# A convolution's first stage written six sweep products later, each of its groups ordered behind the last sweep product

## The chip, the cores and the metric

The kernel runs on one core of one Trainium2 chip. The metric is the device time of one execution in microseconds (us). A comparison with the kernel before is made of runs of both on the same chip.

## What is computed

One layer of a hybrid encoder, for 2048 positions of 1024 channels. RMSNorm and one input projection feed two groups of heads: a long convolution (three streams of 512 channels) and an mLSTM. Their outputs are joined and projected; a cross attention over 256 memory rows and a squared-ReLU network follow. The change touches the convolution:

```python
def _hyena(hy, spec, skip):
    L = hy.shape[1]
    u = hy.astype(jnp.float32)
    z, g1, g2 = u[..., :D_HYENA], u[..., D_HYENA:2 * D_HYENA], u[..., 2 * D_HYENA:]
    for o, gate in enumerate((g1, g2)):
        conv = jnp.fft.irfft(jnp.fft.rfft(z, n=2 * L, axis=1) * spec[:, o], n=2 * L, axis=1)[:, :L]
        z = gate * (conv + z * skip[o].astype(jnp.float32))
    return z

def reference(x, mem, ...):
    u = _rms_norm(h, norm_mix_g[l])
    proj = u @ w_in[l]
    hy = _short_conv_centred(proj[..., :HY_COLS], hy_conv_w[l], hy_conv_b[l])
    spec = _hyena_filter_spectrum(L, ...)
    y_hy = _group_rms_norm(_hyena(hy, spec, hy_skip[l]), hy_norm_g[l], HYENA_GROUPS)
    ...
```

## The kernel before

The input projection runs in "sweeps": a sweep product is a block of 128 output columns by 512 positions, eight blocks of the inner dimension, three matmuls each (`mm3`: high by high, high by low and low by high parts of x, `xh`/`xl`, and of the weights, `wh`/`wl`), so 24 matmuls on TensorE (PE, lines 351, 354, 355). "Natural" tiles do the same with the roles exchanged, for the values and gates. The weights come through SP's queue (`wn`, line 391) and are split on ACT and DVE (line 362). Half of the positions is done first; then x is scaled and split again for the other half (`xt` loads, line 492).

The convolution is a Fourier transform in matmuls, in four stages. The two convolutions, o=0 and o=1, have the same stages:

- First stage, `spectrum`: for each of eight pieces j2, two pairs of matmuls with the constant `f1` (a pair uses both halves of the array; `beside`, lines 177 and 188), copied out (line 918 and its neighbour) and written to the memory tensor `zs` (line 920; one half on SP's queue, the other on ACT's). The input `z` comes from `hy` (line 851).
- Blocks, i = 0 to 15: `zs` is read back across (line 868), with the filter's tile from `fs` (line 860). `response` makes the filter's values (line 875, into the bank `mm`); the data go through `dm` (line 948, into the bank `hy`), are multiplied by the response on ACT, POOL and DVE (lines 950 to 954), and `back` (line 906, by `em`) follows, one item late; the result is written to `zg` (line 910, ACT's queue).
- Inverse: `zg` is read back (line 890) with the gate (line 893), multiplied by `e2` (line 177 through `beside`), and by the gate on DVE (line 968). For o=0 the next first stage follows at once, one item late; for o=1 a norm, then a write to `yh`.

Who stands where: the program is one Python thread, and the framework's scheduler takes, on each engine, among the instructions that it deems ready, the one written first, except where an order is pinned. Each engine then runs its queue in that fixed order, and waits there for what its instruction needs. The order in which the code is written is set by generators: `weave(a, b, wa, wb)` takes turns between the convolution `p.hyena` (weight 279) and the sweeps (weight 499); each `yield` tells how much work the piece behind it is (a sweep product 5.5, a first-stage piece 3.5, a block 4.6). `p.hyena` begins with `yield 6` ahead of its first piece.

`beside` writes the matmuls of a pair: the last one is made first and, with `pin`, kept in program order among the pinned instructions; the others get a high priority and a pinned place. `mm3` keeps the last matmul of a sweep product in `self.last`, and `behind(ins)` adds an order dependency (no semaphore) on it: `ins` may not be put on PE ahead of that matmul. In the kernel before, the filters' opening uses `behind`; `spectrum` does not.

In what follows, a number of sweep matmuls is the count of projection matmuls that PE's queue holds ahead of an instruction.

Of the kernel before, what the change touches and what calls it, by code (L numbers as in the profile page):

```python
# [133 lines left out]
class Prog:  # L134
# [38 lines left out]
    def beside(self, *products, pin=False):  # L173
        names = [p[0].tensor.name for p in products]
        n = min(self.banks.index(t) for t in names)
        held = self.banks[max(0, n - 4):max(0, n - 2)] if len(set(names)) > 1 else []
        b = self.nc.tensor.matmul(*products[-1], start=True, stop=True)  # L177
        if pin:
            self.tc.keep_in_program_order(b)
        for i in reversed(self.nc.cur_bb.bb.instructions[-4000:]):  # L180
            own = [x.bass_ap.tensor.name for x in i.ins if getattr(x, "bass_ap", None) is not None]
            for t in [t for t in held if t in own]:
                held.remove(t)
                self.tc.add_manual_dep(b.ins, i.name, mybir.DependencyInfo(
                    mybir.DependencyClass.Sync, mybir.DependencyReason.DATA), reason="beside")
        with self.tc.high_priority(2000):
            for p in reversed(products[:-1]):
                self.tc.keep_in_program_order(self.nc.tensor.matmul(*p, start=True, stop=True))
# [633 lines left out]
    def hyena(self, es):  # L822
# [6 lines left out]
        own = [slice(64 * g, 64 * g + 64) for g in range(2)]  # L829
# [6 lines left out]
        def ta():  # L836
            return sb.tile([128, 2, CH], F32, tag="a", name="a", bufs=10)
# [4 lines left out]
        f1 = sb.tile([128, 128], F32, name="f1")  # L842
# [4 lines left out]
        def load1(j2):  # L847
            z = ta()
            js = slice(2 * j2, 2 * j2 + 2)
            for g in range(2):  # L850
                nc.sync.dma_start(out=z[own[g]], in_=hy[0, g, :, js])
            return z
# [59 lines left out]
        def spectrum(o, j2, z):  # L912
            st = [ta() for p in range(2)]
            for jj in range(2):
                pp = [self.hy() for b in range(2)]
                self.beside(*((pp[g], f1[own[g]], z[own[g], jj]) for g in range(2)), pin=True)
                for b in range(2):
                    (nc.vector.tensor_copy if b else nc.scalar.copy)(st[b][:, jj], pp[b])
            for b in range(2):
                (nc.sync if b else nc.scalar).dma_start(out=sds[o][b, :, 2 * j2:2 * j2 + 2], in_=st[b])  # L920

        q, fq = [load1(0), load1(1)], []
        yield 6
        for j2 in range(8):
            yield 3.5
            if j2 < 6:
                q.append(load1(j2 + 2))
            else:
                fq.append(load_filter(0, j2 - 6))
            spectrum(0, j2, q.pop(0))  # L930
        for o in range(2):
# [4 lines left out]
            for i in range(16):  # L936
# [9 lines left out]
                for m in range(2):  # L946
                    pp = self.hy()
# [11 lines left out]
            for j2 in range(8):  # L959
                yield 4.5 if o else 6.0  # L960
                js = slice(2 * j2, 2 * j2 + 2)
                r, gate = nxt
                if j2 < 7:
                    nxt = load3(o, j2 + 1)
                for jj in range(2):
                    pp = self.hy()
                    self.beside(*((pp[own[g]], e2, r[g][:, jj]) for g in range(2)), pin=jj == 0)
                    nc.vector.tensor_tensor(gate[:, jj], pp, gate[:, jj], ALU.mult)
                if o == 0:
                    late(lambda j2=j2, gate=gate: spectrum(1, j2, gate))  # L970
                    if j2 > 5:
                        fq.append(load_filter(1, j2 - 6))
                    continue
                y = gate.rearrange("q j (g e) -> q (j g) e", g=8)
                sq = ta()
                sqv = sq.rearrange("q j (g e) -> q (j g) e", g=8)
                nc.gpsimd.tensor_tensor(sqv, y, y, ALU.mult)
                ms = sb.tile([128, 16], F32, tag="ms", name="ms", bufs=2)
                nc.vector.tensor_reduce(ms, sqv, AX.X, ALU.add)
                rv = self.bank_rsqrt(sb, ms, 64)  # L980
                nc.vector.tensor_tensor(sqv, y, rv.unsqueeze(2).broadcast_to([128, 16, 64]), ALU.mult)
                for jj in range(2):
                    nc.gpsimd.tensor_tensor(sq[:, jj], sq[:, jj], ghy, ALU.mult)
                for g in range(2):
                    nc.sync.dma_start(out=yh[g, :, js], in_=sq[own[g]])
# [954 lines left out]
def chain(*gens):  # L1940
    for g in gens:
        yield from g


def weave(a, b, wa, wb, until=False):
    da = db = 0.0
    fa = fb = False
    while not (fa and fb):
        if fb or (not fa and da / wa <= db / wb):
            try:  # L1950
                da += next(a)
            except StopIteration:
                fa = True
        else:
            try:
                db += next(b)
            except StopIteration:
                fb = True
                if until:
                    return  # L1960


def program(p):
    with ExitStack() as ms:
        with ExitStack() as es:
            p.inproj_open(es)
            p.filters_open()
            p.prepq = p.x_first()
            p.pop()
            s = chain(p.sweep(range(4), 0, True, lambda: p.prep_x(1)), p.opened(), p.sweep(range(4), 1, False))  # L1970
            f = p.filters()
            for _ in range(5):
                next(s)
            next(f)
            next(f)
            next(s)
            weave(s, f, 140, 102, True)
            p.gates_open(ms)
            n = p.memproj()
            with ExitStack() as hs:  # L1980
                weave(p.hyena(hs),
                      chain(s, p.sweep(range(4, 10), 1, True), p.natural(1, (3, 0, 1, 2), lambda: p.prep_x(0)),
                            p.natural(0, (3,)), among(p.sweep((4, 5, 8, 9), 0, False), p.gates(), 2),
                            among(chain(p.natural(0, (0, 1)), p.sweep((6, 7), 0, False),
                                        p.natural(0, (2,), p.prep_mem, 2), take(n, 3)), p.states(), 1)),
                      279, 499)
            m = p.mlstm(ms)
            weave(n, take(m, 5), 55, 30)
            for _ in take(m, 1):
                pass  # L1990
        with ExitStack() as rs:
            p.ts = rs.enter_context(ExitStack())
            p.tail_open(p.ts)
            with ExitStack() as at:
                g = p.attention(at)
                weave(g, m, 440, 96, True)
                ms.close()
                p.ffn_open(rs)
                for _ in g:
                    pass  # L2000
            p.ffn()


def among(g, h, every):
    for i, v in enumerate(g):
        yield v
        if i % every == every - 1:
            next(h, None)
    for _ in h:
        pass  # L2010


def take(g, n):
    for _ in range(n):
        v = next(g, None)
        if v is None:
            return
        yield v
# [31 lines left out]
```

## Time and profile before

| what | value |
|---|---|
| runs before, us | 3146.3, 3149.82, 3152.24 (median 3149.82) |
| profiled execution, us | 3143.82 |
| its span, us | 3142.1 |
| mean granted TensorE clock | 0.984 of full speed |
| DMA traffic | 607.13 MB, mean 193 GB/s |

In the profile's lines a name is the program's, without its buffer number; an arrow points from what is read to what is written; L351 is line 351. "SPq" and "ACTq" are the DMA-issuing queues of these engines. In the chain of waits each row is a start, a length and what the end of the program hung on at that time. In a timeline a bracket tells how long the engine stood idle ahead of the row, and which instruction's end let it go on. Matmuls overlap: a 128x512 row takes 0.39 to 0.43 us from start to end, but the next begins 0.23 us after it.

### The profile page before, as it was taken

What the parts mean: (1) busy time and instruction counts of PE and PEld (TensorE: products, weight loads), DVE (VectorE), ACT (ScalarE), POOL (GpSimd) and SP (SyncE); (2) the same over time, 40 slices, a digit from 0 to 9 for tenths busy, and PEclk for the clock granted to TensorE, in tenths of its full rate; (3) what the DMA queues carried; (4) which work ended last, traced back from release to release, by engine and by line L of the source; (5) the groups of instructions that cost most, each with busy time, mean ns of one, the idle gap of its engine ahead of it and who ended that gap; (6) DMA issues with size and microseconds to landing.
All of it is one profiled execution on the core that took longest, in us unless ns stands there. A gap on an engine that the chain in (4) does not pass through costs nothing.

```text
span 3142.1 us, 43602 instructions
## 1 busy us (share of the span) xinstructions
PE 3030.6 (96%) x14481; PEld 2390.2 (76%) x14481; DVE 2049.6 (65%) x3569; ACT 1493.9 (48%) x2848; POOL 1161.9 (37%) x802
## 2 busy tenths in 40 slices
PE   8999999999999977999999999999999999999998
PEld 6655566876687767888887888888888778888876
DVE  7965456446646778877765656557555685555695
ACT  5443366534646345454544455556555443333335
POOL 0122012100222244324141327776456393434493
PEclk9999999999999988999999999999999999999999
DMA  6564767586777987455385647656644574434424
GB/s 212 153 209 164 260 192 214 171 253 216 215 217 233 279 274 254 147 181 196 113 282 165 234 154 245 208 184 225 207 154 151 172 238 144 151 124 152 124 91 171
DMA packets 446667, 607.13 MB, mean 193 GB/s; under 512 B 39007, under 2 KB 249055, under 8 KB 445417
## 3 DMA queue, kind: packets, MB, share of 16 engines
q1 hardware_dynamic: 408548, 546.54, 54.5%
q10 hardware_dynamic: 37892, 57.79, 5.5%
q8 instruction: 115, 1.88, 0.2%
q14 instruction: 112, 0.91, 0.1%
HBM read 401.79 MB, written 202.41 MB: 192 GB/s over the span
## 4 chain that ended last, share of the span: by engine, by line
PE 79%; DMA 8%; DVE 6%; issue 3%; ACT 2%; POOL 1%; SPq 1%; ACTq 0%; DVEq 0%; POOLq 0%
PE mm L351 17%; PE mm L355 17%; PE mm L354 17%; PE hy L355 5%; PE hy L351 5%; PE hy L354 5%; PE hy L177 3%; PE mm L875 2%; PE hy L906 2%; PE hy L948 2%; DMA a<-hy 1%; PE hy L1112 1%; DVE wl L362 1%; PE hy L1235 1%; DVE bl L1580 1%
## 5 line engine op out<-in xcount | busy, mean ns | idle before, releaser
L362 DVE TENSOR_TENSOR wl<-wn,wh 128x512 fp32r<-128x512 f32 (+1 forms) x364 | 285.9, 828 | 120.8 <-ACT wh L362 120.3
L1580 DVE TENSOR_TENSOR bl<-wr,bh 128x512 fp32r<-128x512 f32 x213 | 240.4, 1136 | 132.3 <-ACT bh L1579 132.2
L1579 ACT CAST ah<-w 128x512 fp32r<-128x512 f32 x284 | 177.1, 624 | 301.9 <-PE hy L354 154.5
L953 POOL TENSOR_TENSOR b<-b,a 128x512 f32<-128x512 f32 x64 | 88.5, 1383 | 533.7 <-ACT b L951 507.9
L351 PE MATMUL mm<-xh,wh 128*128 128x512 f32 x640 | 272.9, 427 | 11.2 <-ACT wh L362 9.1
L362 ACT CAST wh<-wn 128x512 fp32r<-128x512 f32 (+1 forms) x364 | 205.3, 620 | 154.6 <-PE mm L355 51.8
L1579 ACT CAST bh<-wr 128x512 fp32r<-128x512 f32 x232 | 143.9, 622 | 237.3 <-PE mm L355 172.6
L355 PE MATMUL mm<-xh,wl 128*128 128x512 f32 x640 | 256.5, 401 | 0.0
L354 PE MATMUL mm<-xl,wh 128*128 128x512 f32 x640 | 255.1, 399 | 0.7 <-DVE xl L362 0.6
L1580 DVE TENSOR_TENSOR al<-w,ah 128x512 fp32r<-128x512 f32 x236 | 215.3, 913 | 54.1 <-ACT ah L1579 54.0
L355 PE MATMUL mm<-bh,al 128*128 128x512 f32 x576 | 224.7, 393 | 6.0 <-DVE al L1580 3.4
L351 PE MATMUL mm<-bh,ah 128*128 128x512 f32 x576 | 226.5, 393 | 2.2 <-DVE acc L1737 2.2
L354 PE MATMUL mm<-bl,ah 128*128 128x512 f32 x576 | 225.7, 392 | 0.0
L351 PE MATMUL mm<-act,wh 128*128 128x512 f32 x512 | 199.2, 395 | 2.1 <-ACT wh L362 2.0
L354 PE MATMUL mm<-act,wh 128*128 128x512 f32 x512 | 200.4, 392 | 0.2 <-DVE act L362 0.2
L355 PE MATMUL mm<-act,wl 128*128 128x512 f32 x512 | 199.7, 392 | 0.9 <-DVE wl L362 0.6
L351 PE MATMUL hy<-bh,ah 128*128 128x512 f32 x448 | 175.2, 391 | 0.0
L354 PE MATMUL hy<-bl,ah 128*128 128x512 f32 x448 | 174.6, 390 | 0.0
L355 PE MATMUL hy<-bh,al 128*128 128x512 f32 x448 | 174.4, 390 | 0.0
L351 PEld LDWEIGHTS mm<-xh,wh 128*128 128x128 f32 x640 | 121.9, 191 | 66.6 <-issue 23.5
L334 POOL TENSOR_TENSOR b<-b 128x512 f32<-128x512 f32 x32 | 58.3, 1823 | 277.2 <-DVE b L331 137.6
L354 PEld LDWEIGHTS mm<-xl,wh 128*128 128x128 f32 x640 | 121.9, 191 | 48.8 <-issue 22.6
(380 smaller groups left out, 8479.3 us busy)
## 6 DMA issues: line engine op xcount, KB each, us to landing
wr<-hc SPq DMA_DIRECT2D x224, 256.0 KB
w<-in_ff_w_dram SPq DMA_DIRECT2D x172, 256.0 KB
hc<-wn SPq DMA_DIRECT2D x128, 256.0 KB
wn<-in_w_in_dram SPq DMA_DIRECT2D x100, 256.0 KB
hc<-q SPq DMA_DIRECT2D x96, 256.0 KB
fs<-a SPq DMA_DIRECT2D x32, 512.0 KB
a<-fs SPq DMA_DIRECT2D x64, 256.0 KB
a<-zs SPq DMA_DIRECT2D x64, 256.0 KB
```

What stands on the lines that cost most here:

```text
L177: b = self.nc.tensor.matmul(*products[-1], start=True, stop=True)
L334: nc.gpsimd.tensor_tensor(e[1], f, b, ALU.subtract)
L351: first = mm(ps, lh, rh, start=start, stop=False)
L354: mm(ps, lh, rl, start=False, stop=False)
L355: self.last = mm(ps, ll, rh, start=False, stop=stop)
L362: both = (self.nc.scalar.copy(hi, src), self.nc.vector.tensor_tensor(lo, src, hi.bitcast(F32), ALU.subtract))
L875: nc.tensor.matmul(pp, dm[:, m], t[:, m], start=True, stop=True)
L906: nc.tensor.matmul(pg, em[:, m], y, start=True, stop=True)
L948: nc.tensor.matmul(pp, dm[:, m], t[:, m], start=True, stop=True)
L953: nc.gpsimd.tensor_tensor(xt, xt, hi[:, m], ALU.mult)
L1579: self.nc.scalar.copy(hi, src)
L1580: eng.tensor_tensor(lo, src, hi.bitcast(F32), ALU.subtract)
```

## The change

```diff
@@ beside
         if pin:
             self.tc.keep_in_program_order(b)
+        if pin == 2:
+            self.behind(b)
@@ hyena
-                self.beside(*((pp[g], f1[own[g]], z[own[g], jj]) for g in range(2)), pin=True)
+                self.beside(*((pp[g], f1[own[g]], z[own[g], jj]) for g in range(2)), pin=1 if o else 2)
...
         q, fq = [load1(0), load1(1)], []
-        yield 6
+        yield 24
@@ program
-                      279, 499)
+                      297, 499)
```

The first stage of the first convolution (o=0) gets the order dependency: the last-written matmul of each pair stands behind the last sweep product that was written ahead of it. The convolution's first piece is written 18 units of its own measure later, and its weight in `weave` goes up by the same 18, so that its end stays beside the same place of the sweeps. No instruction is added or removed on PE, DVE, POOL or the queues; ACT loads an activation table two times more (for Silu and Sigmoid). In the changed kernel all lines from 180 on have a number higher by 2.

On PE, rows differ from sweep matmul 939 to the start of the mLSTM, and nowhere else. The sixteen pairs of the first stage stood in ten places between sweep matmuls 939 and 1021; now they stand two by two at 939, 960, 984, 1008, 1032, 1056, 1080 and 1104. The first response (line 875) stood at 1008, ahead of the last two pairs, and the first line 948 at 1056; now they stand at 1104, right behind the last two pairs, and at 1176. The later blocks of o=0 come 96 to 264 sweep matmuls later, the inverse of o=0 begins at 2165 instead of 2016, the last first-stage piece of o=1 stands at 2579 instead of 2520, the last inverse of o=1 at 3906 instead of 3890.

SP's queue at the handover from first stage to blocks, before (`zs` is the first stage's result, `fs` the filter, `qt` a result of the sweep):

```order
L851 DMA a<-hy 64x1024 x2
L920 DMA zs_2574<-a 128x1024
L757 DMA hy<-st 126x4x128 x2
L860 DMA a<-fs_354 64x2x512 x2
L920 DMA zs_2574<-a 128x1024
L860 DMA a<-fs_354 64x2x512 x2
L920 DMA zs_2574<-a 128x1024 x2
L868 DMA a<-zs_2574 64x2x512 x2
```

and after the change:

```order
L922 DMA zs_2574<-a 128x1024
L768 DMA qt<-cv 128x1008
L393 DMA wn<-in_w_in_dram 128x2x256
L862 DMA a<-fs_354 64x2x512 x2
L393 DMA wn<-in_w_in_dram 128x2x256 x3
L922 DMA zs_2574<-a 128x1024
L768 DMA qt<-cv 128x1008
L862 DMA a<-fs_354 64x2x512 x2
L922 DMA zs_2574<-a 128x1024 x2
```

In both, the first load of `fs` stands behind the fifth write of `zs`; weight loads and a write of `qt` now stand around it, where two writes of `hy` stood.

SP's queue where the inverse of o=0 (`zg`, with its gate from `hy`) meets the loads of x for the other half (`xt`), before:

```order
L890 DMA a<-zg_2576 128x1024 x2
L893 DMA a<-hy 64x1024 x2
L890 DMA a<-zg_2576 128x1024 x2
L893 DMA a<-hy 64x1024 x2
L391 DMA wn<-in_w_in_dram 128x2x256 x4
L890 DMA a<-zg_2576 128x1024 x2
L893 DMA a<-hy 64x1024 x2
L492 DMA xt<-in_x_t_dram 128x2x512 x2
```

and after the change:

```order
L494 DMA xt<-in_x_t_dram 128x2x512 x2
L892 DMA a<-zg_2576 128x1024 x2
L895 DMA a<-hy 64x1024 x2
L892 DMA a<-zg_2576 128x1024 x2
L895 DMA a<-hy 64x1024 x2
L494 DMA xt<-in_x_t_dram 128x2x512
L892 DMA a<-zg_2576 128x1024 x2
L895 DMA a<-hy 64x1024 x2
```

The first two `xt` loads have moved from behind the third step's loads to ahead of the first's.

PE's queue at sweep matmul 1368, in the middle of the blocks of o=0 and between two natural tiles, before (`b` is the product with the response; lines 774 and 784 are transposes of a sweep's result):

```order
L355 MATMUL mm<-wh,xl 128x272
L774 MATMUL mm<-ident,cv 128x128 x7
L906 MATMUL hy<-b,em 128x512
L948 MATMUL hy<-a,dm 128x512
L784 MATMUL mm<-ident,cv 112x128
L351 MATMUL mm<-wh,xh 128x272
```

and after the change:

```order
L357 MATMUL mm<-wh,xl 128x272
L908 MATMUL hy<-b,em 128x512
L950 MATMUL hy<-a,dm 128x512
L776 MATMUL mm<-ident,cv 128x128 x4
L908 MATMUL hy<-b,em 128x512
L950 MATMUL hy<-a,dm 128x512
L776 MATMUL mm<-ident,cv 128x128 x3
L908 MATMUL hy<-b,em 128x512
L950 MATMUL hy<-a,dm 128x512
L786 MATMUL mm<-ident,cv 112x128
L353 MATMUL mm<-wh,xh 128x272
```

Three pairs of lines 908 and 950 stand between the two tiles, where one pair stood and two more came at matmul 1392.

## The prediction

> **What bounds the kernel now.** I read the page's first part, then its chain of waits, to see which engine sets the end.
>
> ```profile
> span 3142.1 us, 43602 instructions
> PE 3030.6 (96%) x14481; PEld 2390.2 (76%) x14481; DVE 2049.6 (65%) x3569; ACT 1493.9 (48%) x2848; POOL 1161.9 (37%) x802
> PE 79%; DMA 8%; DVE 6%; issue 3%; ACT 2%; POOL 1%; SPq 1%; ACTq 0%; DVEq 0%; POOLq 0%
> ```
>
> TensorE (PE) is busy for 3030.6 of 3142.1 us. No matmul is added or dropped, so the time can move only through the 111.5 us in which PE stands idle, through the clock that it is granted, and through what it pays when it changes from one kind of matmul to another. The change first alters PE's order at about 352 us and last at about 1200 us. So I went along PE's timeline of that stretch, one idle place after the other. The costliest one within the convolution lies where its first stage hands over to its spectral blocks; this is the chain of waits there (start, length, what):
>
> ```profile
> 352.97 0.62 PE hy L177
> 353.60 0.42 PE hy L177
> 354.88 0.43 PE mm L351
> 355.31 0.23 PE mm L354
> ...
> 384.88 5.89 DMA a<-fs
> 390.91 3.75 PE mm L875 x4
> ...
> 400.12 0.68 DVE a L918
> 400.82 3.90 DMA zs<-a
> ...
> 404.78 0.58 SPq L868
> ...
> 405.47 4.64 DMA a<-zs
> 410.24 1.95 PE hy L948 x4
> ```
>
> and this is the idle time of PE there, from its timeline (in brackets the idle time before the row, and who ended it):
>
> ```profile
> 390.91 3.75 PE L875 MATMUL mm<-a,dm 128*128 128x512 f32 x4 [4.70 <-DMA a<-fs]
> 410.24 1.95 PE L948 MATMUL hy<-a,dm 128*128 128x512 f32 x4 [1.16 <-DMA a<-zs]
> ```
>
> Two transfers are late: the filter tile fs, 4.70 us, and the first stage's own result, zs, written to memory and read back, 1.16 us. Four matmuls of the same line take 1.72 us elsewhere and 3.75 us behind the 4.70 us gap:
>
> ```profile
> 510.90 1.72 PE mm L875 x4
> ```
>
> **First handover.** In the changed order the L875 that needs fs stands right behind the last of eight first-stage groups, which are now one sweep product (24 matmuls) apart. The loads of fs leave SP's queue some two products earlier, between the fifth and sixth write of zs, and no longer right ahead of their use. Let T be the time at which PE has three products and four groups left before that L875. Ahead of the load SP's queue then holds the fifth write of zs (its group ends at T+1.9, its copy 0.7 later), a write of qt, which the copies of one product feed, and one weight load; I estimate that it goes at T+8. With 5.89 us of transfer it lands at T+14, and even at twice that length at T+20. PE comes there after 3 x 24 x 0.23 = 16.6 us of products and four groups of 2.1 us (next paragraph): T+25. So the wait of 4.70 us goes, and with it the slow stretch, 3.75 - 1.72 = 2.03 us. The reload of zs takes 0.68 + 3.90 + 0.58 + 4.64 and some 0.3 us of steps between, 10.1 us. Before, 35 sweep matmuls (8.0 us) and two L875 (0.9) covered it but for 1.16 us; now 72 matmuls (16.6 us) and four L875 (1.7 us) do, 18.3 us. The 1.16 us goes, and 0.23 us of the four L948, 1.95 - 1.72. Together 4.70 + 2.03 + 1.16 + 0.23 = 8.1 us, plus 0.3 us for a slowed first sweep matmul after the gap, **-8.4 us**. Its bounds are -9 and, should the wait for zs stay, -7.0. What the held groups cost in themselves is nothing: the order dependency makes no engine wait for a signal, and both sides stand on PE's queue. What queues behind a group is the next sweep product, which was on PE anyway.
>
> A group's first matmul takes 0.62 instead of 0.42 us, and the first sweep matmul behind it 0.43 instead of 0.23: a change of kind costs 0.4 us. The sixteen pairs stood in ten places and now stand in eight: **-0.8 us**. A group of two pairs, which is four rows in the chain, so adds 0.62 + 3 x 0.42 + 0.2 = 2.1 us between two products.
>
> **Second handover.** The same chain in the second convolution, with its rows:
>
> ```profile
> 777.99 0.69 DVE a L918
> 778.69 3.71 DMA zs<-a
> ...
> 782.44 0.59 SPq L868
> ...
> 783.12 0.91 SPq L1078
> ...
> 784.13 3.65 DMA a<-zs
> 787.82 3.47 PE hy L948 x4
> ```
>
> ```profile
> 787.82 3.47 PE L948 MATMUL hy<-a,dm 128*128 128x512 f32 x4 [2.58 <-DMA a<-zs]
> ```
>
> From 777.99 to 787.82 are 9.8 us; PE had work for 7.25 of them. In the changed order about 10.1 us of matmuls lie there. If all holds, 2.58 us and the slow four, 3.47 - 1.72 = 1.75 us, are gone: -4.3. If the load meets one more transfer, nothing is. I take **-2.5**, since cover and chain are nearly equal; bounds -4.3 and 0.
>
> The Trainium skill, "TensorE: Matmul & The Clock Gate", Part 1, says that the clock is halved after an idle window of about 3.4 us, and that the windows run freely, so where one falls is chance. The 4.70 us gap with its slow four agrees; the 2.58 us gap is shorter than such a window and yet the four behind it were slow. By the rule alone the 1.75 us would not be counted, and the sum below would be about 1 us less of a gain.
>
> **Preparing x for the other half.** Between 667 and 691 us PE waits for x, which is scaled and split again on ACT and DVE, and for the inverse's gate:
>
> ```profile
> 667.01 0.69 PE L177 MATMUL hy<-a,f 64*128 64x512 f32 x1 [1.12 <-DVE a L968]
> 671.08 0.40 PE L355 MATMUL mm<-wh,xl 128*128 128x272 f32 x1 [0.61 <-DVE xl L362]
> 681.89 0.39 PE L355 MATMUL mm<-wh,xl 128*128 128x272 f32 x1 [0.62 <-DVE xl L362]
> 684.46 0.69 PE L177 MATMUL hy<-a,f 64*128 64x512 f32 x1 [0.59 <-DVE a L968]
> 688.85 0.39 PE L351 MATMUL mm<-wh,xh 128*128 128x272 f32 x1 [1.55 <-ACT xh L362]
> 690.86 0.39 PE L355 MATMUL mm<-wh,xl 128*128 128x272 f32 x1 [0.99 <-DVE xl L362]
> ```
>
> That is 5.48 us. The inverse of the first convolution now comes up to 150 matmuls later, so the two L177 waits, 1.71 us, lose their place: their gate has been multiplied by then. The x waits, 3.77 us, stay, as the same splits stand ahead of the same products; but the loads of x now lie among the inverse's loads in another order. I take **-1.5**, bounds -4.5 (nearly all gone) and +1.5 (one more wait like the longest).
>
> **Crowded blocks.** The spectral blocks of the first convolution now follow each other faster, by 297 to 279. At one place (the PE rows shown last with the change) three pairs of L906 and L948 stand between two tiles where one stood. An L906 needs what the L948 before the one just ahead of it gave, through ACT, POOL and DVE. The rows of that place:
>
> ```profile
> 522.23 1.02 PE L948 MATMUL hy<-a,dm 128*128 128x512 f32 x2
> 522.53 0.59 ACT L950 ACTIVATE b<-hy 64x512 f32<-64x512 f32 x1
> 523.79 1.30 POOL L953 TENSOR_TENSOR b<-b,a 128x512 f32<-128x512 f32 x1 [13.16 <-ACT b L951]
> 526.20 0.68 DVE L954 TENSOR_TENSOR b<-b 128x512 f32<-128x512 f32 x1
> 527.99 3.94 POOL L953 TENSOR_TENSOR b<-b,a 128x512 f32<-128x512 f32 x2 [2.90 <-PE mm L774]
> 532.53 1.13 PE L906 MATMUL hy<-b,em 128*128 128x512 f32 x2 [0.48 <-DVE b L954]
> ```
>
> The bare chain is two copies on ACT (0.59 each), 1.30 on POOL and 0.68 on DVE, 3.2 us, and about 4 with the steps between. The second L906 has some 2 us less of PE work ahead than that chain and its queues take, the third 1.6, and the following transposes and tile about 1.3 together: 4.9, less the 0.48 that is there now, **+4.5 us**. If the queues are empty it is 0; if both waits last as long as POOL's pair (3.94), about +7.
>
> **End of the convolution.** The last inverse and its norm slide by 16 to 22 sweep matmuls, into a stretch in which transfers already set the pace (columns: stretch, length, busy time of PE, PEld, DVE, ACT, POOL, granted clock, share of the DMA engines, GB/s):
>
> ```profile
> 350.00:400.00 50.00, 45.30 (x180) 26.01 (x179) 19.10 (x29) 16.60 (x27) 0.00 (x0) 0.93 0.92 307
> 1040.00:1080.00 40.00, 32.90 (x220) 27.24 (x219) 27.55 (x57) 11.90 (x22) 11.08 (x7) 0.94 1.00 303
> 1080.00:1120.00 40.00, 37.04 (x242) 28.82 (x241) 36.98 (x81) 15.51 (x30) 17.45 (x11) 0.94 1.03 332
> ```
>
> One step of the inverse moves two zg tiles, a gate and a result, by their shapes 2 MB; some 0.6 of a step enters the stretch, 1.3 MB, at 303 GB/s 4 us if nothing hides it. The inverse also leaves the place that it had, so I take **+1.5**, bounds -1 and +4. Two more loads of an activation table on ACT lie in an engine that is busy 48%; they cost PE nothing unless a copy that it waits for stands behind one, about 1 us each.
>
> The Trainium skill, "DMA: Bandwidth & Descriptors", Issuing engines are not separate DMA queues, says that transfers started from different engines share the same 16 DMA engines. At a share of 1.00 the rows bear it out: work moved to ACT's queue would be no escape here. By it alone the +4 end would hold.
>
> **The sum.** -8.4 - 0.8 - 2.5 - 1.5 + 4.5 + 1.5 = -7.2 us. The profiled execution took 3143.82 us (span 3142.1), so that one would take 3136.6. The median of the runs shown, 3149.82, is 6.0 above it; off the median the sum gives 3142.6, and I say 3143. A difference of 0.2%, 6.3 us, is about what a measurement can tell from none.
>
> **Rivals.**
> First, no change (3149): the fs wait is only shifted. For it speaks the share of 0.92 in the stretch 350 to 400, where the queue is full: should fs land 11 us later than reckoned, at T+25, it is late again, and crowded blocks take back what is left. Against it: the eight first-stage groups are spread over seven products now, where ten stood within three and a half, so fewer bytes are asked for per us.
> Second, slower (3157): the loads of x behind the inverse's. Both go through SP's queue, one after the other. In the old order the loads of three steps of the inverse stand ahead of the first x load, long before x is needed; in the new one the inverse starts inside the x preparation, at sweep matmul 2165 instead of 2016, and each x load but the first has one or two steps in front, each 1.5 MB by the shapes. Two steps, 3 MB, at 0.3 MB per us (the 307 GB/s above) are 10 us; PE would wait those, and after a gap above 2.6 us run its next matmuls slowly, 2 us more. With this -7.2 + 1.5 + 10 + 2 is about +7. It decides once the x loads come some 3 us later than PE now gets them, the wait of 1.55 us being the margin. Against it: x is loaded a chunk ahead, and the first load now precedes the inverse's.
> Third, a larger gain (3135): both handovers vanish wholly (-4.3 rather than -2.5) and the crowded blocks wait nowhere: -7.2 - 1.8 - 4.5 = -13.5, so 3136 off the median, and a little less with the x waits gone. For it: POOL and ACT are idle for long in that stretch.
>
> **Chances.** The forecast 0.55, no change 0.13, slower 0.20, larger gain 0.12. The forecast's own range, from the root of the squared half widths of its terms (1, 3, 2, 3.5, 2.5: about 6) and 3 us for the median itself, is 3136 to 3150; a little over half of it lies past the 0.2% bound. So faster 0.33 + 0.12 = 0.45, same 0.20 + 0.13 = 0.33, slower 0.02 + 0.20 = 0.22. The range is 3132 to 3157: its low end takes in most of the larger gain, its high end half of the slower case.
>
> **What would show it.** In the changed profile: no idle time before the first L877 (the old L875) and its four matmuls near 1.7 us; no wait for zs before the first L950; granted clock 1.00 in that stretch. Between 500 and 545 us two or three waits of L908 (old L906) on DVE, 1 to 2 us each. From 660 to 700 us waits for x of about 4 us in total; more than 10 means the second rival. Around 790 us a wait for zs of 0 to 2.6 us. From 1040 to 1170 us waits for wh and wl as long as now within 4 us. The prediction is wrong if a wait for fs of over 2 us is still there, if the table loads or queues put new waits into the sweep products, or if the later half, whose order is unchanged, moves by more than 3 us.

## The result, and the profile after

The changed kernel takes 3157.86 us (median of 9 runs, 3154.41 to 3164.36), the kernel before 3146.3 us (9 runs, 3140.25 to 3152.24): a ratio of 1.0037, 95% interval 1.0024 to 1.0049. It is slower by 0.37%, some 11.6 us, where 3143 us and a small gain were forecast. The profiled execution's span grew by 10.6 us, from 3142.1 to 3152.7. The page after:

```profile
span 3152.7 us, 43607 instructions
PE 3025.2 (96%) x14481; PEld 2387.8 (76%) x14481; DVE 2063.3 (65%) x3569; ACT 1489.4 (47%) x2846; POOL 1152.8 (37%) x802
PE 80%; DVE 7%; DMA 6%; issue 3%; ACT 2%; POOL 1%; SPq 0%; ACTq 0%; DVEq 0%; POOLq 0%
```

PE is busy 5.4 us less than before, and the span is longer. So it waits more, in all 16 us. Where, the waits alone do not tell well, since other work stands at other places now. I therefore lined the two traces up by the count of sweep matmuls. For each kernel I took the start of every matmul on PE, and subtracted what the rows ahead of it take at their usual pace (the median distance to the next row, for each line and shape, over both traces). What is left is time lost up to there, to waits, a slow clock and changes of kind. This table gives the lost time in a stretch of sweep matmuls, less that of the kernel before in the same stretch:

```
stretch (sweep matmuls)  what lies there                      lost against before, us
0 to 900                 ahead of the first moved row                -0.9
900 to 1200              first stage, first handover                 -9.7
1200 to 1600             blocks of o=0, crowded                      +1.2
1600 to 2100             blocks of o=0                               -0.2
2100 to 2450             inverse of o=0, x for the other half        +8.8
2450 to 2850             second handover                             -3.2
2850 to 3200             blocks of o=1                                0.0
3200 to 4064             last inverse, memory projection             +2.3
4064 to 4410             opening of the mLSTM                       +14.6
4410 to the end          the rest                                    -2.3
sum                                                                 +10.6
```

It compares one profiled execution of each kernel. The changed kernel's, 3154.41 us, is the shortest of its nine runs.

**First handover.** PE's timeline after, at the rows that waited before:

```profile
407.94 1.98 PE L877 MATMUL mm<-a,dm 128*128 128x512 f32 x4
427.84 1.88 PE L950 MATMUL hy<-a,dm 128*128 128x512 f32 x4
```

No bracket, so no wait, and four matmuls take 1.9 us rather than 3.75. The stretch from 350 to 400 us has PE busy throughout, at full clock, with the DMA engines as full as before (columns as in the prediction):

```profile
350.00:400.00 50.00, 50.00 (x222) 34.16 (x220) 25.09 (x38) 23.90 (x37) 0.00 (x0) 1.00 0.93 287
```

**Crowded blocks and second handover.** Of the three L908 that the prediction looked at, one waits; at the second handover the wait for `zs` is shorter than before (2.58 us), and no slow four follow it:

```profile
505.31 1.10 PE L908 MATMUL hy<-b,em 128*128 128x512 f32 x2 [1.36 <-DVE b L956]
...
803.32 1.95 PE L950 MATMUL hy<-a,dm 128*128 128x512 f32 x4 [1.00 <-DMA a<-zs]
```

**The x stretch.** The two longest waits of PE's timeline there, and the chain of waits that leads to the first:

```profile
672.08 0.60 PE L353 MATMUL mm<-wh,xh 128*128 128x272 f32 x1 [7.16 <-ACT xh L364]
689.58 0.40 PE L353 MATMUL mm<-wh,xh 128*128 128x272 f32 x1 [1.94 <-ACT xh L364]
```

```profile
654.48 9.30 DMA xt<-in_x_t_dram
663.79 7.20 DMA wn<-in_w_in_dram
670.99 1.04 ACT xh L364
```

One load of x, 512 KB, takes 9.30 us. It is not the whole of the 7.16 us: ACT comes to the split late for another reason too, and the row of `wn` in this chain is only what the profile names for that (e7 and e9 below show ACT's queue). Why the load is late, SP's queue tells:

```profile
647.47 1.78 SPq L892 DMA_DIRECT2D a<-zg  x2
649.30 1.14 SPq L895 DMA_DIRECT2D a<-hy  x2
650.48 1.06 SPq L892 DMA_DIRECT2D a<-zg  x2
651.58 1.09 SPq L895 DMA_DIRECT2D a<-hy  x2
654.48 0.39 SPq L494 DMA_DIRECT2D xt<-in_x_t_dram  x1
655.44 1.34 SPq L892 DMA_DIRECT2D a<-zg  x2
```

Two steps of the inverse, 3 MB by the shapes, were issued in the seven microseconds ahead of it, and another step right behind. That these loads make it late was still a theory here; e3 tests it. In the kernel before, the nearest step lay nine microseconds ahead of the first pair of x loads:

```profile
647.17 0.81 SPq L890 DMA_DIRECT2D a<-zg  x2
...
656.55 4.46 SPq L492 DMA_DIRECT2D xt<-in_x_t_dram  x2
```

**The opening of the mLSTM**, which the prediction had left out. PE's two longest waits there, after:

```profile
1178.01 2.04 PE L1199 MATMUL hy<-qn,kk_t 128*128 128x128 f32 x8 [7.05 <-DMA kk_t<-kt]
1225.48 2.06 PE L1114 MATMUL hy<-ve,kn 128*128 128x129 f32 x8 [9.05 <-issue]
```

"issue" means that the profile shows nothing that PE waited for. The rows of DVE ahead of that place do: L1114 needs a bank that DVE has to empty, and DVE stands still for 7.23 us until a write of `ym` has landed, whose source it is about to overwrite:

```profile
1224.95 0.76 DVE L1250 TENSOR_TENSOR ht<-hy,den 128x256 f32<-128x256 f32 x2 [7.23 <-DMA ym<-ht]
```

The same two rows before, of PE and of DVE:

```profile
1214.10 2.06 PE L1112 MATMUL hy<-ve,kn 128*128 128x129 f32 x8 [3.23 <-ACT rw L1206]
```

```profile
1213.58 0.76 DVE L1248 TENSOR_TENSOR ht<-hy,den 128x256 f32<-128x256 f32 x2 [1.69 <-DMA ym<-ht]
```

And SP's queue, first after, then before (`acc` is 1 MB a load, the residual for the attention that follows):

```profile
1212.06 1.76 SPq L1368 DMA_DIRECT2D wn<-yh  x4
1213.86 0.98 SPq L1401 DMA_DIRECT2D acc<-in_x_t_dram  x2
1214.94 1.83 SPq L1274 DMA_DIRECT2D ym<-ht  x2
1216.86 0.54 SPq L1102 DMA_DIRECT2D va<-vd  x1
```

```profile
1207.04 1.28 SPq L1366 DMA_DIRECT2D wn<-yh  x3
1208.37 0.43 SPq L1272 DMA_DIRECT2D ym<-ht  x1
1208.84 0.43 SPq L1366 DMA_DIRECT2D wn<-yh  x1
1209.37 0.43 SPq L1272 DMA_DIRECT2D ym<-ht  x1
1209.85 0.50 SPq L1399 DMA_DIRECT2D acc<-in_x_t_dram  x1
```

Before, both `ym` writes went out ahead of `acc`; after, both `acc` loads, 2 MB, go out ahead of them. A write issued at 1214.94 us keeps DVE waiting until 1224.95, 10.0 us; before, one issued at 1208.37 did so until 1213.58, 5.2 us. Why the order turned over is not shown; probably `acc`, with everything else some microseconds later, was ready sooner than `ym` by the scheduler's own reckoning.

### The profile page after: what moved, and what is told of

It reads as the page before. It is cut to its first block, busy times and chain, and to the rows that moved or that the text cites. A ratio compares the mean times of both kernels' runs of the same rounds, so it can differ in the third digit from the quotient of the medians.

```text
span 3152.7 us, 43607 instructions
## 1 busy us (share of the span) xinstructions
PE 3025.2 (96%) x14481; PEld 2387.8 (76%) x14481; DVE 2063.3 (65%) x3569; ACT 1489.4 (47%) x2846; POOL 1152.8 (37%) x802
## 4 chain that ended last, share of the span: by engine, by line
PE 80%; DVE 7%; DMA 6%; issue 3%; ACT 2%; POOL 1%; SPq 0%; ACTq 0%; DVEq 0%; POOLq 0%
PE mm L353 17%; PE mm L357 17%; PE mm L356 17%; PE hy L357 5%; PE hy L353 5%; PE hy L356 5%; PE hy L177 3%; PE mm L877 2%; PE hy L908 1%; PE hy L950 1%; DVE wl L364 1%; DVE bl L1582 1%; DMA xt<-in_x_t_dram 1%; PE hy L1237 1%; PE hy L1114 1%
## 5 line engine op out<-in xcount | busy, mean ns | idle before, releaser
L353 PE MATMUL mm<-xh,wh 128*128 128x512 f32 x640 | 268.0, 420 | 11.6 <-ACT wh L364 9.1
L353 PE MATMUL mm<-wh,xh 128*128 128x256 f32 (+1 forms) x512 | 156.8, 307 | 14.2 <-ACT xh L364 9.1
```

The lines of the kernel that those rows point to most:

```text
L353: first = mm(ps, lh, rh, start=start, stop=False)
```

## The experiments

**What the order tells without a run.** With the order dependency alone (yield 6, weight 279) every engine's instructions stand in the order of the kernel before, row by row; without it (yield 24, weight 297, `pin=True`) in that of the changed kernel. The scheduler had placed the groups no earlier by itself. So the dependency does nothing here; the change is the later writing and the weight.

The theory to be tested, formed from the two traces: the gain lies at the first handover, and two losses come from the order of loads and writes on SP's queue, at x and at the mLSTM's opening (theory A for the latter). Its rival: the loss goes with the lateness of the convolution as such. The table gives all runs, by the stretches of above (the last two taken together, since the half versions mix them otherwise); the ratio is to the kernel before, run beside them.

```
run                  900-   1200-  2100-  2450-  3200-   ratio   95% interval
                     1200   2100   2450   2850   4410
changed kernel       -9.7   +1.0   +8.8   -3.2  +16.9   1.0037  1.0024 to 1.0049
e1 weight 301        -9.7   +2.1  +11.7   +4.2   -5.3   1.0008  0.9997 to 1.0019
e2 acc behind ym     -9.7   +1.0  +11.9   -3.3   +2.3   1.0016  1.0004 to 1.0029
e3 x first           -9.7   +1.0   -2.2   +0.4  +11.2   0.9997  0.9983 to 1.0011
e4 half              -8.0   -0.6   +5.3   -5.2   +2.1   0.9973  0.9964 to 0.9982
e5 x first and acc   -9.7   +1.0   -4.0   -0.1   +7.9   0.9978  0.9969 to 0.9988
e6 half, x first 14  -8.0   -0.5   +3.5   -3.7   -2.0   0.9960  0.9946 to 0.9974
e7 od off ACT, other tiles  -9.7   +1.0  +14.5   -3.4   +9.8   1.0017  1.0005 to 1.0029
e8 before, fs early  +3.4   -0.3   -2.4   +0.7   +6.6   1.0026  1.0017 to 1.0036
e9 od off ACT        -9.7   +1.0   +9.8   -2.8  +14.0   1.0036  1.0022 to 1.0050
e10 half, x first 18 -8.0   +0.1   -0.7   +1.1   -2.3   0.9966  0.9957 to 0.9976
```

Each row is one profiled execution. e1, e2 and e7 have SP's order of the changed kernel at x, and lose 11.7, 11.9 and 14.5 there, it 8.8: so the figures of that stretch spread by up to 6 us with the order unchanged.

### e1: another weight

```diff
-                      297, 499)
+                      301, 499)
```

> The changed kernel with 301 in place of 297 as the convolution's weight. The first handover and the loads of x keep their order; on SP's queue at the opening of the mLSTM the two acc loads (1 MB each) now stand behind two ym writes and a cbn and a va load, where in the changed kernel they stand ahead of them. Theory A (the mLSTM's opening is lost to the acc loads ahead of ym and va): the 9.05 us idle before the second line L1114 there is under 3 us, the opening loses about 4 us against the kernel before where the changed one loses 12, and the whole is 2 to 5 us above the kernel before. Rival B (the convolution's late end pushes the opening back, whatever the queue's order): the opening loses 12 us as now, the whole is about 11 us above.

PE at the opening of the mLSTM:

```profile
1214.97 2.06 PE L1114 MATMUL hy<-ve,kn 128*128 128x129 f32 x8 [1.63 <-issue]
```

The wait of 9.05 is 1.63 us, and the last two stretches lose 5.3 us less than before, where the changed kernel loses 16.9 more. The first handover keeps its gain and x its loss, and the whole is 0.08% over the kernel before, about 2.5 us. Theory A holds so far, but the weight also shifted the second handover (+4.2), so e1 is no clean proof.

### e2: acc behind ym

```diff
-                nc.sync.dma_start(out=acc[:, 4 * h:4 * h + 4], in_=src)
+                d = nc.sync.dma_start(out=acc[:, 4 * h:4 * h + 4], in_=src)
+                for w in self.yms[:2] if c == 0 else []:
+                    tc.add_manual_dep(d.ins, w.ins.name, mybir.DependencyInfo(
+                        mybir.DependencyClass.NoSync, mybir.DependencyReason.DATA), reason="after ym")
```

(`self.yms` collects the writes of `ym`.)

> The changed kernel, with an order dependency that puts the first two acc loads behind the first two ym writes on SP's queue; nothing ahead of that place is moved. Theory A: everything up to the opening of the mLSTM loses what the changed kernel loses, and from there 7 to 9 us come back: the whole is 2 to 5 us above the kernel before. Rival B: under 2 us come back.

SP's queue and PE's timeline:

```profile
1212.70 1.28 SPq L1275 DMA_DIRECT2D ym<-ht  x2
1214.03 0.50 SPq L1402 DMA_DIRECT2D acc<-in_x_t_dram  x1
```

```profile
1178.11 2.04 PE L1200 MATMUL hy<-qn,kk_t 128*128 128x128 f32 x8 [6.91 <-DMA kk_t<-kt]
...
1217.76 2.06 PE L1115 MATMUL hy<-ve,kn 128*128 128x129 f32 x8 [1.98 <-ACT rw L1209]
```

The convolution is as late as in the changed kernel, `kk_t` is as late (6.91 and 7.05 us), and yet the opening (sweep matmul 4064 to 4410) loses 3.1 us instead of 14.6: 11.5 come back, where 7 to 9 were expected. The table's 3200 to 4410 falls by more, 14.6, but 3 us of that lie ahead of the place that the edit touches. The profiled execution is also the shortest of its ten runs; by the ratio, which falls from 1.0037 to 1.0016, 6.6 us come back, and the whole is 5.0 us over the kernel before, as theory A had it. Rival B, under 2 us back, is out.

The other runs fit. In the four kernels with both `acc` loads ahead of the two `ym` writes (changed, e3, e8, e9), PE waits 6.75 to 9.05 us at this instruction; in before, e1, e2 and e5, with both `ym` writes ahead, it waits 0.99 to 3.23 us.

### e3: x first

```diff
+                if o == 0:
+                    tc.add_manual_dep(d.ins, self.xdma.ins.name, mybir.DependencyInfo(
+                        mybir.DependencyClass.NoSync, mybir.DependencyReason.DATA), reason="after x")
...
+            if o == 0:
+                yield 14
             nxt = load3(o, 0)
...
-                yield 4.5 if o else 6.0
+                yield 4.5 if o else 4.25
```

(`d` is the load of `zg`, `self.xdma` the last load of x.)

> The changed kernel, with the inverse of the first convolution written 14 units later and its zg loads ordered behind the loads of x, so that all eight x loads are issued ahead of the inverse's loads; the inverse's steps follow faster by as much, and the opening of the mLSTM keeps its order on SP's queue. Theory (the x stretch is lost because x loads share the queue and the transfers with the inverse's loads, and ACT's queue waits for these): the 7.16 us idle before a tile's first matmul on xh goes, the stretch from sweep matmul 2100 to 2450 loses no more than in the kernel before (8 us), where the changed one loses 16; the whole is 2 to 5 us above the kernel before. Rival (x is late for a reason of its own, such as the splits on ACT and DVE): at least 5 us of the 8 stay. Second rival: the inverse now waits for zg itself, and the loss moves to the second handover, by 3 us or more.

SP's queue:

```profile
645.00 9.24 SPq L494 DMA_DIRECT2D xt<-in_x_t_dram  x3
655.79 2.18 SPq L393 DMA_DIRECT2D wn<-in_w_in_dram  x4
659.12 4.04 SPq L494 DMA_DIRECT2D xt<-in_x_t_dram  x2
...
668.34 0.38 SPq L494 DMA_DIRECT2D xt<-in_x_t_dram  x1
668.77 0.93 SPq L892 DMA_DIRECT2D a<-zg  x2
```

All loads of x stand ahead of the inverse's, and x costs 2.2 us less than in the kernel before instead of 8.8 more. By the packets in the traces, the third and fourth of the six loads of x that are issued from 640 us on have their last packet 3.2 and 5.0 us after the issue, where the changed kernel's take 7.9 and 10.0. Of the second rival there is a trace: the second handover gains nothing now (+0.4, where the changed kernel had -3.2). `acc` still stands ahead of `ym`, and PE waits 6.75 us there; but of the 11.2 us in the table 8.5 lie ahead of the opening, between sweep matmul 3200 and 4064, and no run shows why. The whole is 0.9 us under the kernel before, where 2 to 5 above were expected. The edit also writes the inverse 14 units later, so order and lateness change together here.

### e4: half of the change

```diff
-        yield 24
+        yield 15
...
-                      297, 499)
+                      288, 499)
```

> Yield 15 and weight 288: half of the change. First-stage groups up to sweep matmul 1056, the first line 948 72 matmuls behind the L875, as in the changed kernel. On SP's queue three steps of the inverse stand ahead of the first x load, as in the kernel before, and the acc loads stand behind ym and va. If the loss sits in those two orders and the gain in the cover of 72 matmuls: gain of 6 to 10 us at the first handover kept, no loss at x beyond 3 us and none at the mLSTM's opening beyond 4 us, the whole 2 to 10 us under the kernel before. If the loss goes with the lateness as such: half of the gain and half of the loss, about 5 us above.

8.5 us under the kernel before, as the first theory had it, and not half-way between gain and loss. x misses its bound: +5.3 where at most 3 were expected, though three steps of the inverse are ahead of the first load of x as before. The order is the same, but the distance is not. The third step's last loads start 4.6 us ahead of the first two of x, where the kernel before had 8.4; DVE waits for x until 656.96 us, 8.95 after the issue, and PE behind it:

```profile
643.46 1.68 SPq L895 DMA_DIRECT2D a<-hy  x2
648.01 1.53 SPq L494 DMA_DIRECT2D xt<-in_x_t_dram  x2
...
656.96 2.74 DVE L483 SCALAR_TENSOR_TENSOR xt<-xt,par,rb 128x512 f32<-128x512 f32 x4 [4.11 <-DMA xt<-in_x_t_dram]
659.51 0.59 PE L353 MATMUL mm<-wh,xh 128*128 128x272 f32 x1 [4.01 <-ACT xh L364]
```

### e5: both repairs

The edits of e2 and e3 together.

> Both repairs in the changed kernel: x loads ahead of the inverse's loads, and the acc loads behind the first two ym writes. If each takes back its own place: the first handover keeps its gain of 9.7 us, the x stretch loses nothing (0 to -3 us against the kernel before), the end of the convolution and the opening of the mLSTM together lose 0 to 5 where the changed kernel loses 17: the whole 4 to 12 us under the kernel before. Rival: the two repairs meet the same loss (the opening was late because x was late), and the whole is as with x first alone, within 2 us of the kernel before.

0.22% under the kernel before, 6.9 us, within what was expected; the two losses are separate ones. The last stretches lose 7.9 rather than 0 to 5; 6.0 of that lie between sweep matmul 3200 and 4064, ahead of the opening, as in e3, and the cause is open.

### e6 and e10: half of the change, x first

The edits of e4 and e3; the yield ahead of the inverse is 14 in e6 and 18 in e10 (with 4.25 and 3.75 per step).

> Yield 15 and weight 288, with the inverse of the first convolution 14 units later and its loads behind those of x (one step of it still ahead of the third x load). The acc loads stand behind the ym writes without help. If the x loss of 5 us in that half version goes as it did in the whole one: 8 us gained at the first handover, 0 to -3 us at x, the whole 9 to 14 us under the kernel before, the fastest of all. Rival: the second handover, which gained 5 us in the half version, loses its cover as the inverse is packed closer, and the whole stays at 5 to 8 under.

> As e6 (yield 15, weight 288), with the inverse 18 units later rather than 14, so that all x loads are issued ahead of all its loads. If the 3.5 us that e6 still loses at x come from the one step that stood ahead of the third x load, as they did not in the whole version with x first: x at 0 to -4 us, the whole 10 to 15 us under the kernel before. If they have another cause, or the closer inverse takes them back: the same as e6 within 2 us.

e6 is 12.6 us under the kernel before, the fastest of all with e10 (10.7 us; the intervals overlap). By one profiled execution each, both answers of e10 are true: x loses nothing once all its loads are ahead (-0.7 for +3.5), and the inverse, pressed closer, gives the gain of the second handover back (+1.1 for -3.7). The difference at x is smaller than the spread there.

### e7 and e9: a write that holds ACT

In the changed kernel's trace the load of x has landed at 663.8 us, but ACT splits it at 671.0, behind a write of `od` in its queue that is issued at 667.8, as a load of `zg` lands. That write waits, by its own list of semaphores, for that load: both count on the same one. Two more such writes follow before the split:

```profile
663.80 1.41 DVE L483 SCALAR_TENSOR_TENSOR xt<-xt,par,rb 128x512 f32<-128x512 f32 x2 [4.19 <-DMA xt<-in_x_t_dram]
667.83 0.33 ACTq L817 DMA_DIRECT2D od<-st  x1
670.07 0.81 ACTq L817 DMA_DIRECT2D od<-st  x2
670.98 1.05 ACT L364 CAST xh<-xt 128x1024 fp32r<-128x1024 f32 x1 [2.07 <-DMA wn<-in_w_in_dram]
```

x is scaled by 665.2 us, so some 5.8 of PE's 7.16 us are ACT's delay, and the rest the load's. e7 moved the writes to POOL, but those of other tiles (PE's wait stays, at 7.66 us), so it tells nothing of this; e9 moved the right ones:

```diff
-                nc.scalar.dma_start(out=(self.d_vd if c2 < 2 else self.d_od)[r0:r0 + 128, ...
+                (nc.gpsimd if hf == 0 and c2 == 3 else nc.scalar).dma_start(out=(self.d_vd if c2 < 2 else self.d_od)[r0:r0 + 128, ...
```

(e7: `hf == 1 and c2 == 2`.)

> The changed kernel with the od writes of the eight tiles around the x stretch issued by POOL in place of ACT; the order of loads of zg and x on SP's queue there is the same. If ACT's split of x was late mainly because an od write ahead of it in ACT's queue waited for the landing of a zg load: the longest idle time before a tile's first matmul on xh falls from 7.16 us to under 3 us. If the x load itself is what is late: it stays above 5 us. The opening of the mLSTM is ordered anew by this, so the whole says nothing.

> The writes that e7 meant: the changed kernel with the od writes of the tiles that run in the x stretch (first half of the positions, last column block) issued by POOL in place of ACT; SP's queue keeps its order at x and at the opening of the mLSTM. In the changed kernel's trace the load of x lands at 663.8 us, but ACT's split of it starts at 671.0, behind an od write that goes at 667.8, as a zg load ends. If that write is what holds the split: the idle time of 7.16 us before the tile's first matmul on xh falls to 1 to 4 us, and 4 to 7 of the 9 to 12 us lost between matmul 2100 and 2450 come back. If the x load alone is late: it stays above 5 us.

PE's timeline of e9, and the piece of its chain of waits:

```profile
671.73 0.39 PE L357 MATMUL mm<-wh,xl 128*128 128x272 f32 x1 [0.50 <-DVE xl L364]
679.09 0.59 PE L353 MATMUL mm<-wh,xh 128*128 128x272 f32 x1 [5.04 <-DVE sg L821]
```

```profile
666.93 9.99 DMA xt<-in_x_t_dram
676.94 1.42 DVE xt L483 x2
```

The wait of 7.16 us is gone, and the next load of x, 9.99 us long, makes PE wait 5.04 us at the tile after: DVE, which has to empty PE's bank by line 821, stands at the scaling of that x. The stretch loses 9.8 us, within the 8.8 to 14.5 of the four kernels with the write in place, and the 4 to 7 us that were expected back do not show; the whole, 1.0036, is that of the changed kernel. So the semaphore did hold ACT, but without that hold the loss stays, and it is gone where e3 takes the loads of x out from among those of the inverse.

### e8: the kernel before, with its fs loads early

```diff
-            else:
-                fq.append(load_filter(0, j2 - 6))
+            if j2 in (3, 5):
+                fq.append(load_filter(0, (j2 - 3) // 2))
```

> The kernel before, with the two fs loads written behind the fourth and sixth first-stage piece rather than the seventh and eighth, so that they are issued earlier on SP's queue; the first stage and the blocks stay where they are. If the 4.70 us wait and the slow matmuls behind it come from the late issue of that load alone: 6 to 7 us are gained at the first handover, and the wait for zs grows by up to 2 us. As a side effect the acc loads stand ahead of the ym writes at the opening of the mLSTM, with all that leads up to it as in the kernel before: if theory A holds, 6 to 12 us are lost there, and the whole is 0 to 6 us above the kernel before; if the order on that queue is harmless by itself, the whole is 5 to 7 us under it.

PE's timeline at the handover, and at the opening of the mLSTM:

```profile
405.00 1.12 PE L875 MATMUL mm<-a,dm 128*128 128x512 f32 x2 [1.66 <-ACT P L717]
413.42 3.75 PE L948 MATMUL hy<-a,dm 128*128 128x512 f32 x4 [7.29 <-DMA a<-zs]
...
1224.67 2.06 PE L1112 MATMUL hy<-ve,kn 128*128 128x129 f32 x8 [7.88 <-issue]
```

The wait for `fs` is gone, as meant, but that for `zs` grows from 1.16 to 7.29 us with a slow four behind it: 3.4 us lost where 6 to 7 gained were expected. An early load alone doesn't make the gain; it needs the 72 matmuls between the last group and the L950 as well. The opening is the mirror of e2: the convolution there is as early as in the kernel before, but `acc` stands ahead of `ym`, and 6.6 us are lost, with 7.88 of waiting at the same instruction. The whole is 8.2 us above the kernel before (1.0026), more than the 0 to 6 that were expected, as the first handover loses too. Theory A holds in both directions.

## Why the prediction was wrong, point by point

- **First handover and changes of kind**, -8.4 and -0.8: measured -9.7. Right, with its reason: neither `fs` nor `zs` is waited for, the four L877 take 1.98 us, the clock is granted in full. That the groups stand apart comes from the later writing; the order dependency of the title changes no engine's order. e8 adds what the prediction had as two terms side by side: without the longer cover of `zs`, the gain on `fs` would have been lost again.
- **Crowded blocks**, +4.5: measured +1.2 (up to matmul 1600). The mechanism was right, but only one L908 waits, 1.36 us, where the sum priced two of them and what follows at 4.9; the other pairs hardly wait.
- **Second handover**, -2.5: measured -3.2. Right: the wait for `zs` is 1.00 us, and the four behind it are not slow.
- **Preparing x**, -1.5, bounds -4.5 and +1.5: measured +8.8. Here a step failed. The prediction said that the x waits stay "as the same splits stand ahead of the same products" and for the loads that they wait for, which it saw in another order, it allowed one more wait of 1.55 us at most. What happened is in the main the second rival, which had 0.20: x loads behind one or two steps of the inverse. It reckoned 10 us of waiting and 2 of slow matmuls; the load took 9.30 us, and the stretch lost 8.8. It did not see that ACT's split would also be held by a write in its queue, some 5.8 us of the longest wait. The rows to price the loads were at hand, SP's order and 307 GB/s.
- **End of the convolution**, +1.5: measured +2.3, within its bounds; but e2, with the same order up to there, has -0.8, so the stretch can't tell this from nothing. One premise was false: ACT loads an activation table two times fewer, not two times more: 10 times in the trace where it was 12.
- **The mLSTM's opening**, no term at all: measured +14.6. This is the larger failure, and the reason why the time lies outside the range. The prediction let the change end where PE's order ceases to differ, "at about 1200 us", and asked of SP's queue only at the handovers and at x. SP's order differs at 1212 us too: two `acc` loads stand ahead of two `ym` writes. DVE waits 7.23 us for such a write to land, and PE 9.05 us for DVE, a wait that PE's own timeline does not name. e2 takes 11.5 of the 14.6 us back with this order alone (6.6 by the ratio of the whole), and e8 loses 6.6 by it in the kernel before. The prediction's own sign, a later half that moves by more than 3 us, was the right one to watch.

That the slower rival's 3157 lies within 1 us of the measured 3157.86 is luck. Its sum comes to +6.3, put down as +7, all of it at x, and it starts from a median of 3149.82 where the nine runs beside the changed kernel have 3146.3; measured are +11.6, and the larger part of the loss lies at the opening, which it did not have.

Of what the Trainium skill was cited for, "TensorE: Matmul & The Clock Gate", Part 1, has more rows now: four matmuls take 3.75 us behind a wait of 7.29 in e8, as behind 4.70 before, which its window of about 3.4 us allows for. The slow four behind the 2.58 us gap ran at half the clock too: the trace of the kernel before grants 0.50 from 789.6 to 791.3 us, as from 390 to 394 us behind the 4.70 us gap. So a gap shorter than that window was enough here, and by the measurement the prediction was right to count the 1.75 us; behind the 1.00 us of the changed kernel the clock is granted in full. Where the limit lies, no run settles. What "DMA: Bandwidth & Descriptors" says in Issuing engines are not separate DMA queues agrees with e9: with the write moved to another engine, the loads of x took as long.

What stays open: why PE waits 7 us for `kk_t` in the changed kernel and e2, where it waited 3.78 us for `cbn` before (the queue ahead of it holds two more weight loads and a late write of `yh`; no run took these alone away); what e3 and e5 lose between sweep matmul 3200 and 4064; and whether more distance alone, with the order of e4, would free its loads of x.

## What to carry to other kernels

A change that moves a block of work in time moves the order of every queue behind it, also where the bounding engine's order is the same: compare the DMA queues to the end of the program before a stretch is called unchanged. A large load that nobody waits for yet, ahead of a small write or load that someone does, can hold that one up: here a `ym` write by about 5 us, a load of x by as much. One order dependency between the two (e2, 6.6 us by the ratio) or loads put ahead (e3, 11 us in its stretch) gave most of it back. And half of a move can be worth more than all of it: the gain needed 72 matmuls of cover, which the half version had too.

## What the runs showed of the hardware that was not expected

Two `ym` writes issued behind 2 MB of `acc` and 1 MB of `yh` loads held DVE until 10.0 us after the first was issued, against 5.2 where the acc loads came behind them; 9.4 to 10.0 in the four kernels with `acc` ahead (changed, e3, e8, e9), 3.1 to 5.2 in before, e1, e2 and e5. And a write in ACT's queue stood 8 us, and a split behind it with it, because its completion semaphore was that of a load issued from SP's queue that had not landed.
